# Weighed queries times both states as plain float32 products, without the splits of states and queries

## The chip, the core and the metric

The kernel runs on one core of a Trainium2 chip. Its engines are TensorE (PE, with its weight loads as PEld), VectorE (DVE), ScalarE (ACT), GpSimd (POOL) and SyncE (SP, which issues most DMAs). The metric is the device time of one execution in microseconds (us); lower is better.

## What is computed

One encoder block on x of 2048 tokens by 1024 channels: a norm, one input projection, two branches (a pooling mixer and a bidirectional mLSTM), a gate by SiLU for each, one output projection, the residual and a last norm. The change lies in the mLSTM. It has 4 heads of 256 channels and works in 16 chunks of 128 tokens, in two directions, with a state C (256 x 256) and n (256) that goes from chunk to chunk:

```python
def step(carry, xs):
    C, n, m = carry
    ...
    s = jnp.einsum('bhtd,bhsd->bhts', qj, kj) * jnp.exp(log_D - m_t[..., None])
    num = jnp.einsum('bhts,bhse->bhte', s, vj) + inter_w[..., None] * jnp.einsum('bhtd,bhde->bhte', qj, C)
    den = jnp.sum(s, axis=-1) + inter_w * jnp.einsum('bhtd,bhd->bht', qj, n)
    h = num / jnp.maximum(jnp.abs(den), jnp.exp(-m_t))[..., None]
    ...
    C_new = decay[..., None, None] * C + jnp.einsum('bhs,bhsd,bhse->bhde', ws, kj, vj)
```

## The kernel before

Most products are split: a float32 operand is cast to a high part of type fp32r, the low part is what is left, and a product of two operands becomes three one-pass products (high x high, high x low, low x high), summed in PSUM. Some products are plain float32 instead, among them the scores of the mLSTM (`sT`) and the headwise maps (`hw`).

The program has an input stage (all projections and small maps, results to DRAM), then the z blocks and the pooled branch, and then the mLSTM as a pipeline of 64 steps: step s is head h = s // 16, chunk j = s % 16 of the forward direction. The states of the backward direction are made one head ahead, one update for each step, and held in `cb`; the forward state is `cf`. Between the pieces of a step stand "fill" units, three passes each of the output projection (`po`).

A step uses these pieces. `weigh` multiplies the queries c by the weights of both states, for two directions and two halves of 128 channels (`cw`, on GpSimd). `weighed_high` and `weighed_low` split it (`cwh` on ScalarE, `cwl` on GpSimd). `state_high` and `state_low` split the state of direction d: `sh` on ScalarE, `sl` on DVE for the forward state (d = 0) and on GpSimd for the backward one (d = 1). `numerators` sums, per direction, the scores' part (`ph`, `pl` times `vh`, `vl`) and the states' part in one PSUM tile `num`, 258 columns wide. `denominators`, `ratio`, `moments`, `normalise`, `transposes`, `join`, `store` follow (`rn`, `hh`, `rstd`, `py`, `yt`). `forward` and `backward` update the states: six products into the PSUM tile `upd`, then DVE adds the decayed state (`cf`, `cb`). `upd` has one buffer (`psu`) for both directions, `cw` has two (`tp`).

The table `order` says what is done in iteration s, in the order of every engine: a piece, how many iterations it lags behind its step (`weigh` with -2 makes `cw` of step s + 2, `numerators` with 0 is step s) and sometimes the engine. For iterations up to 52 TensorE, DVE, ScalarE and GpSimd run exactly in this order; for the last steps the framework's scheduler orders all but TensorE. The first 53 iterations hold some five fill units each, later ones sixteen or fewer (`share`, `units`).

Of the kernel before, what the change touches and what calls it, by code (L numbers as in the profile page):

```python
# [10 lines left out]
F32 = mybir.dt.float32  # L11
# [6 lines left out]
P = 128  # L18
# [32 lines left out]
def hymba_block(ctx, tc, xT, x, w_in, wpxT, pool_w, bqT, bkT, bvT, bv, w_g, b_g, par, edge, w_out, g_out, out):  # L51
# [27 lines left out]
    # gate products that the recurrences use, token-major: column r = (dir, step, head)  # L79
# [16 lines left out]
    # ------------------------------------------------------------------ input projections  # L96
# [26 lines left out]
    # from the last z blocks on, TensorE runs in the order of the program  # L123
# [15 lines left out]
    # the small operands of the headwise maps, read ahead  # L139
# [3 lines left out]
    def load_headwise(i):  # L143
        t = {}
        for name, src in (("k", bkT), ("v", bvT)):
            t[name] = hwp.tile([P, P], F32, name=f"bl{name}")
            nc.sync.dma_start(out=t[name], in_=src[i])
        # the map of q and, beside it, the gates' weights of k, q and v
        t["q"] = hwp.tile([P, P + 48], F32, name="blq")
        nc.sync.dma_start(out=t["q"][:, :P], in_=bqT[i])  # L150
        nc.sync.dma_start(out=t["q"][:, P:].rearrange("p (a b) -> p a b", a=3), in_=w_g[i])
        t["vw"] = hwp.tile([P, 16 + P], F32, name="vw")
        nc.sync.dma_start(out=t["vw"][:, 16:], in_=bv[i])
        return t
# [6 lines left out]
    # W_poolx times the group's mix: pooling commutes with the mix of the channels  # L161
# [44 lines left out]
    with ExitStack() as pro:  # L206
        xq = open_pool(pro, "xq", bufs=2)

        # u is x g in two parts that one pass each carries; the row factor 1 / rms multiplies the products
# [40 lines left out]
        # the array's clock rises while the first loads run  # L250
# [38 lines left out]
    # ---- the mLSTM's inputs  # L289
    with pm:  # L290
# [5 lines left out]
        def prepare(i):  # L296
            bl, vw = hw[i], hw[i]["vw"]
            wq = bl["q"]
            # the columns of a map: what it adds to the gates, then its outputs
# [21 lines left out]
        def headwise(i, b):  # L321
# [3 lines left out]
            for src, off, rhs, dst in ((c, 0, mws[i], kk_s), (mxs[i], 2 + b * BT, hw[i]["vw"], v_s)):  # L325
                # v's columns end with ones, whose product with the keys is the denominator, and a pad
# [85 lines left out]
    # ---- z of the mLSTM (first heads) beside the gates: columns of gacc are (i|f, dir, head)  # L412
    with ExitStack() as pz:
# [31 lines left out]
        # in the order (dir, step, head)  # L445
# [15 lines left out]
        # rows r, columns t  # L461
# [34 lines left out]
        flat = lambda t: t.rearrange("p a b c -> p (a b c)")  # noqa: E731  # L496
# [30 lines left out]
    # ---- the pooling mixer  # L527
# [43 lines left out]
    # ------------------------------------------------------------------ mLSTM  # L571
# [9 lines left out]
    # keys and values of chunk j, and their parts; the keys carry the weights of the state's update  # L581
# [7 lines left out]
    # pieces of the split of keys and values  # L589
# [36 lines left out]
    # the state that chunk j - 1 receives from its right  # L626
# [25 lines left out]
    # ---- the output projection: units of three products, and chores that go between them  # L652
# [67 lines left out]
    def fillers():  # L720
        # the first and the last tiles go in pairs by halves of the columns, while the other half's weights come
# [9 lines left out]
        def ahead(i):  # L731
            # reads y of piece i when it can be had
            if i < len(pieces) and keys[i] not in ys and (pieces[i][0] == 0 or pieces[i][2] in done):
                ys[keys[i]] = load_y(*keys[i])
# [44 lines left out]
    # ---- a step of the forward direction, in pieces that go to different engines  # L779
# [20 lines left out]
    def mask(a):  # L800
        # keys s (partitions) that a query t may see: s <= t forward, s >= t backward
        for d, (pat, cm) in enumerate(((1, -1), (-1, 1))):
            nc.gpsimd.affine_select(out=a["gw"][:, 0, d, :], in_=a["gw"][:, 0, d, :], compare_op=ALU.is_ge, fill=BIG,
                                    base=0, pattern=[[pat, P]], channel_multiplier=cm)

    # c times the weights of the states, and its parts
# [5 lines left out]

    def weighed_high(a):
        a["cwh"] = tp.tile([P, 2, 2, P], F32R, name="cwh")
        nc.scalar.copy(a["cwh"][:, a["ds"]], a["cw"][:, a["ds"]])  # L815

    def weighed_low(a, eng):
        ds = a["ds"]
        a["cwl"] = tp.tile([P, 2, 2, P], F32R, name="cwl")
        eng.tensor_tensor(a["cwl"][:, ds], a["cw"][:, ds], a["cwh"][:, ds].bitcast(F32), op=ALU.subtract)  # L820
# [24 lines left out]
    def numerators(a):  # L845
# [6 lines left out]
        for d in a["dirs"][::-1]:  # L852
            sh, sl = a["sh", d], a["sl", d]
            for m in range(2):
                for n, (l, r) in enumerate((("cwh", sh), ("cwh", sl), ("cwl", sh))):
                    pe(nc.tensor.matmul(num[:, d, :E], lhsT=a[l][:, d, m, :], rhs=r[:, m, :],
                                        start=False, stop=(m == 1 and n == 2)))

    # the parts of the state that step a meets in direction d
    def state_high(a, d):  # L860
        if d in a["dirs"]:
            a["state", d] = cb.pop((a["h"], a["j"])) if d else a["cf"]
            a["sh", d] = fp.tile([P, 2, E], F32R, name=f"sh{d}", bufs=1)
            nc.scalar.copy(a["sh", d], a["state", d])  # L864

    def state_low(a, d, eng):
        if d in a["dirs"]:
            a["sl", d] = fp.tile([P, 2, E], F32R, name=f"sl{d}", bufs=1)
            eng.tensor_tensor(a["sl", d], a["state", d], a["sh", d].bitcast(F32), op=ALU.subtract)  # L869
# [72 lines left out]
    # most of the pooled half's products go evenly into the first FULL steps  # L942
# [9 lines left out]
    def behind(s):  # L952
        # the backward update of the next head that goes with step s
# [3 lines left out]
    # ---- z of the last heads, beside the first backward states; each block that is done makes room  # L957
    for pair in ((4,), (5,), (6, 7)):
# [29 lines left out]
    # The steps run as a pipeline. What is done in iteration s, in the order of every engine: a piece, how many  # L988
    # iterations it lags behind its step, and for some the engine
    V, G = nc.vector, nc.gpsimd  # L990
    order = (
        ("store", 3, V), ("scores_low", 0, G), ("denominators_2", 1), ("state_high_0", 0), ("ratio_0", 1),
        ("forward", 0), ("back_values_high", -1), ("state_low_0", 0, V), ("ratio_1", 1), ("normalise_1", 2),
        ("fill", 0), ("fill", 0), ("state_low_1", 0, G), ("moments_0", 1), ("weighed_low", 0, G), ("fill", 0),
# [4 lines left out]
        ("back_values_low", -1, V), ("skip", 1), ("denominators_1", 0), ("weighed_high", -1), ("state_high_1", -1),  # L999
        ("scores_high", -1),  # L1000
# [4 lines left out]
        mask=mask, weigh=weigh, weighed_high=weighed_high, weighed_low=weighed_low, exponentials=exponentials,  # L1005
# [3 lines left out]
    for n, piece in (("state_high", state_high), ("state_low", state_low), ("denominators", denominators),  # L1009
                     ("moments", moments), ("normalise", normalise)):  # L1010
# [4 lines left out]
    def run(span):  # L1015
        for s in span:
# [7 lines left out]
            # products of the output projection that go into this iteration  # L1024
# [31 lines left out]
# ---- layout of the inputs, and the launch on one core  # L1056
# [48 lines left out]
```

## Time and profile before

| | us |
|---|---|
| three runs | 1572.33, 1572.82, 1577.58 (median 1572.82) |
| profiled execution: span from the first to the last instruction | 1570.6 |
| what lies around the span, against the median | 2.2 |
| busy in the span: PE | 1477.8 (94%) |
| PEld | 1257.9 (80%) |
| DVE | 1034.2 (66%) |
| ACT | 650.6 (41%) |
| POOL | 624.6 (40%) |

Busy time is the time in which an engine has an instruction at work, its waits for a memory port included. Matmuls are pipelined: one's end overlaps the next, so the distance from start to start is what a product costs in a row, and the busy time of a lone matmul is longer. The stages differ much in which engine is full; a share over the whole span mixes them.

### The profile page before, as it was taken

The page shows a single profiled execution, that of the slowest core. Times are in us where ns is not written, and L with a number is a line of the kernel's source. Part 1 is how long each engine was busy: PE and PEld are TensorE (multiplying, and loading weights), DVE is VectorE, ACT ScalarE, POOL GpSimd, SP SyncE. Part 2 cuts the span into 40 slices and gives each one's busy share as a digit, 9 for nine tenths or more (in the row PEclk, how much of TensorE's full clock was granted, in tenths as well). Part 3 has the DMA queues.
Part 4 walks back from the last instruction along what each step waited for, and adds up shares of the span by engine and source line. Part 5 has one row for each costly group of instructions (what it writes and reads, how often), then busy time and mean ns, then how long its engine had stood idle before and what let it go on. Part 6 is the DMA issues. An engine that isn't in the chain of part 4 may idle for free.

```text
span 1570.6 us, 23151 instructions
## 1 busy us (share of the span) xinstructions
PE 1477.8 (94%) x7801; PEld 1257.9 (80%) x7801; DVE 1034.2 (66%) x1993; ACT 650.6 (41%) x1516; POOL 624.6 (40%) x752
## 2 busy tenths in 40 slices
PE   8899999999999999999999888888888899899998
PEld 6689888878888888888887777777777777787886
DVE  8795445562134333434543999999999999766753
ACT  6245443442011110001234666666666666635431
POOL 6543333310000222221020777777767778443300
PEclk9999999999999999999999999999999999999999
DMA  6268766542111101111337776676676667754352
GB/s 218 73 201 242 184 182 177 167 143 77 55 54 54 54 16 52 54 54 54 101 108 226 235 200 185 203 207 189 193 208 192 187 202 239 203 181 154 119 163 81
DMA packets 251351, 231.25 MB, mean 147 GB/s; under 512 B 18400, under 2 KB 211168, under 8 KB 250208
## 3 DMA queue, kind: packets, MB, share of 16 engines
q1 hardware_dynamic: 236768, 215.08, 45.9%
q10 hardware_dynamic: 14464, 14.68, 3.0%
q8 instruction: 62, 1.02, 0.3%
q14 instruction: 57, 0.47, 0.1%
HBM read 149.81 MB, written 79.89 MB: 146 GB/s over the span
## 4 chain that ended last, share of the span: by engine, by line
PE 56%; DVE 22%; DMA 8%; POOL 6%; issue 5%; ACT 3%; SPq 1%; POOLq 0%; DVEq 0%; ACTq 0%
PE proj L135 40%; PE po L704 7%; PE hw L336 4%; DVE yt L936 3%; DVE rstd L907 2%; DVE vl L605 2%; DMA gw<-g_s 2%; DVE cb L622 1%; DMA ym_s<-yt 1%; DVE yt L931 1%; PE hw L185 1%; DVE sl L869 1%; POOL cwl L820 1%; DVE kl L596 1%; POOL cw L810 1%
## 5 line engine op out<-in xcount | busy, mean ns | idle before, releaser
L135 PE MATMUL proj<-uh,whi 128*128 128x512 f32 x1024 | 403.8, 395 | 4.6 <-DVE mx L204 3.6
L135 PE MATMUL proj<-ul,whi 128*128 128x512 f32 x1024 | 401.5, 392 | 1.5 <-DVE ul L218 1.5
L135 PE MATMUL proj<-uh,wlo 128*128 128x512 f32 x1024 | 401.8, 393 | 0.4 <-DVE wlo L94 0.4
L135 PEld LDWEIGHTS proj<-uh,whi 128*128 128x128 f32 x1024 | 193.7, 189 | 43.3 <-DVE mx L204 3.7
L135 PEld LDWEIGHTS proj<-uh,wlo 128*128 128x128 f32 x1024 | 193.4, 189 | 41.7 <-DVE wlo L94 0.8
L135 PEld LDWEIGHTS proj<-ul,whi 128*128 128x128 f32 x1024 | 193.6, 189 | 40.9 <-DVE ul L218 2.6
L704 PE MATMUL po<-woh,yh 128*128 128x512 f32 x512 | 205.7, 402 | 3.2 <-DVE o L707 1.8
L704 PE MATMUL po<-woh,yl 128*128 128x512 f32 x512 | 202.4, 395 | 2.3 <-DVE yl L94 2.3
L704 PE MATMUL po<-wol,yh 128*128 128x512 f32 x512 | 202.0, 395 | 1.2 <-DVE wol L94 1.2
L91 ACT CAST whi<-wl 128x1024 fp32r<-128x1024 f32 x31 | 32.6, 1052 | 228.7 <-PE proj L135 225.5
L704 PEld LDWEIGHTS po<-woh,yl 128*128 128x128 f32 x512 | 96.6, 189 | 25.2 <-DVE yl L94 3.1
L616 PE MATMUL upd<-vh,kh 128*128 128x258 f32 x240 | 72.6, 302 | 46.8 <-ACT vh L601 45.1
L704 PEld LDWEIGHTS po<-woh,yh 128*128 128x128 f32 x512 | 96.7, 189 | 22.3 <-DVE o L707 2.4
L704 PEld LDWEIGHTS po<-wol,yh 128*128 128x128 f32 x512 | 96.8, 189 | 19.2 <-DVE wol L94 1.5
L316 DVE SCALAR_TENSOR_TENSOR c<-mx,par_sb,c 128x512 f32<-128x512 f32 x128 | 103.4, 825 | 3.0
L543 DVE TENSOR_TENSOR ux<-proj,rnorm 128x512 f32<-128x512 f32 x32 | 22.1, 691 | 124.7 <-PE proj L135 124.7
L869 POOL TENSOR_TENSOR sl<-cb,sh 128x516 fp32r<-128x516 f32 x60 | 86.5, 1441 | 29.9 <-ACT sh L864 25.4
L810 POOL TENSOR_TENSOR cw<-cT,gw 128x512 f32<-128x512 f32 (+1 forms) x64 | 91.8, 1434 | 7.8 <-DMA gw<-g_s 5.7
L556 POOL TENSOR_TENSOR win<-ux 128x2063 f32<-128x2063 f32 x8 | 29.0, 3624 | 160.7 <-DVE ux L543 160.7
L820 POOL TENSOR_TENSOR cwl<-cw,cwh 128x512 fp32r<-128x512 f32 (+1 forms) x64 | 90.3, 1411 | 6.4 <-ACT cwh L815 4.9
L616 PEld LDWEIGHTS upd<-vh,kh 128*128 128x128 f32 x240 | 45.2, 188 | 55.9 <-ACT hh L884 51.5
L843 POOL TENSOR_TENSOR pl<-dd,ph 128x256 fp32r<-128x256 f32 x64 | 51.4, 804 | 87.4 <-ACT ph L839 87.4
(216 smaller groups left out, 3187.4 us busy)
## 6 DMA issues: line engine op xcount, KB each, us to landing
gw<-g_s SPq DMA_DIRECT2D x128, 128.0 KB, 4.4
v<-v_s SPq DMA_DIRECT2D x124, 129.0 KB, 3.4
kk<-kk_s SPq DMA_DIRECT2D x124, 128.0 KB, 3.6
wl<-in_w_in SPq DMA_DIRECT2D x23, 512.0 KB, 3.9
xt<-in_xT SPq DMA_DIRECT2D x32, 256.0 KB, 4.1
cT_s<-c SPq DMA_DIRECT2D x32, 256.0 KB, 3.6
kk_s<-tokst SPq DMA_DIRECT2D x32, 256.0 KB, 2.6
kkT_s<-kkTb SPq DMA_DIRECT2D x32, 256.0 KB, 4.1
```

The costliest lines, as they stand in the source:

```text
L91: nc.scalar.copy(hi, src)
L135: pe(nc.tensor.matmul(ps, lhsT=l[:, kt, :], rhs=r[:, kt, :], start=(kt == 0 and n == 0), stop=(kt == KT - 1 and n == 2)))
L316: nc.vector.scalar_tensor_tensor(c, in0=mx[:, b * BT + t:(b + 1) * BT + t], scalar=par_sb[:, i, t:t + 1], in1=c, op0=ALU.mult, op1=ALU.add)
L336: nc.tensor.matmul(ps[:, e, :], lhsT=src[:, o:o + P], rhs=rhs, start=True, stop=True)
L605: eng.tensor_tensor(t["vl"], t["v"], t["vh"].bitcast(F32), op=ALU.subtract)
L616: pe(nc.tensor.matmul(ps[:, m, :E], lhsT=t[l][:, ms], rhs=t[r_], start=(n == 0), stop=(n == 2)))
L704: pe(nc.tensor.matmul(ps, lhsT=l[:, kt, :], rhs=r, start=(kt == 0 and e == 0), stop=(kt == 7 and e == 2)))
L810: eng.tensor_tensor(a["cw"][:, ds], a["cT"][:, None].broadcast_to([P, nd, 2, P]), a["gw"][:, 1, ds, None, :].broadcast_to([P, nd, 2, P]), ...
L820: eng.tensor_tensor(a["cwl"][:, ds], a["cw"][:, ds], a["cwh"][:, ds].bitcast(F32), op=ALU.subtract)
L843: eng.tensor_tensor(a["pl"], a["dd"], a["ph"].bitcast(F32), op=ALU.subtract)
L869: eng.tensor_tensor(a["sl", d], a["state", d], a["sh", d].bitcast(F32), op=ALU.subtract)
L936: eng.tensor_tensor(yt, yt, a["sz"], op=ALU.mult)
```

## The change

`numerators` multiplies `cw` and the states themselves, as plain float32 products, two for a direction (one for each half). The casts and subtractions that split them are gone from `order` and from the program. Nothing else of the table is moved; the rest of the diff takes out comments.

```diff
-    def weighed_high(a):
-        a["cwh"] = tp.tile([P, 2, 2, P], F32R, name="cwh")
-        nc.scalar.copy(a["cwh"][:, a["ds"]], a["cw"][:, a["ds"]])
-
-    def weighed_low(a, eng):
-        ds = a["ds"]
-        a["cwl"] = tp.tile([P, 2, 2, P], F32R, name="cwl")
-        eng.tensor_tensor(a["cwl"][:, ds], a["cw"][:, ds], a["cwh"][:, ds].bitcast(F32), op=ALU.subtract)
...
         for d in a["dirs"][::-1]:
-            sh, sl = a["sh", d], a["sl", d]
+            state = cb.pop((a["h"], a["j"])) if d else a["cf"]
             for m in range(2):
-                for n, (l, r) in enumerate((("cwh", sh), ("cwh", sl), ("cwl", sh))):
-                    pe(nc.tensor.matmul(num[:, d, :E], lhsT=a[l][:, d, m, :], rhs=r[:, m, :],
-                                        start=False, stop=(m == 1 and n == 2)))
-
-    # the parts of the state that step a meets in direction d
-    def state_high(a, d):
-        if d in a["dirs"]:
-            a["state", d] = cb.pop((a["h"], a["j"])) if d else a["cf"]
-            a["sh", d] = fp.tile([P, 2, E], F32R, name=f"sh{d}", bufs=1)
-            nc.scalar.copy(a["sh", d], a["state", d])
-
-    def state_low(a, d, eng):
-        if d in a["dirs"]:
-            a["sl", d] = fp.tile([P, 2, E], F32R, name=f"sl{d}", bufs=1)
-            eng.tensor_tensor(a["sl", d], a["state", d], a["sh", d].bitcast(F32), op=ALU.subtract)
+                pe(nc.tensor.matmul(num[:, d, :E], lhsT=a["cw"][:, d, m, :], rhs=state[:, m, :],
+                                    start=False, stop=(m == 1)))
...
-        ("store", 3, V), ("scores_low", 0, G), ("denominators_2", 1), ("state_high_0", 0), ("ratio_0", 1),
...
+        ("store", 3, V), ("scores_low", 0, G), ("denominators_2", 1), ("ratio_0", 1),
...
```

The programs of both kernels show where instructions now stand. GpSimd in a step of the pipeline's middle, before; `[waits ...]` names the engines and DMA queues that an instruction waits for, and the PE that `sl` waits for is the last reader of the part of the state that it replaces:

```order
L843 TENSOR_TENSOR pl<-dd,ph 128x256 [waits Activation_49]
L869 TENSOR_TENSOR sl_9902<-cb,sh_9856 128x516 [waits PE_49]
L820 TENSOR_TENSOR cwl<-cw,cwh 128x512
L803 AFFINE_SELECT gw<-gw 128x128 [waits DMAHW4_49]
L803 AFFINE_SELECT gw<-gw 128x128
L902 TENSOR_TENSOR rstd<-rstd,mhalf 128x1 [waits DVE_49]
L810 TENSOR_TENSOR cw<-cT,gw 128x512 [waits DMAHW7_49,Pool_49]
```

GpSimd in a like step of the changed kernel (`pl` is now line 834, the power for `rstd` line 880):

```order
L803 AFFINE_SELECT gw<-gw 128x128 [waits DMAHW2_49]
L803 AFFINE_SELECT gw<-gw 128x128
L880 TENSOR_TENSOR rstd<-rstd,mhalf 128x1 [waits DVE_49,Pool_49]
L810 TENSOR_TENSOR cw<-cT,gw 128x512 [waits DMAHW4_49,DMAHW5_49,PE_49,Pool_49]
L834 TENSOR_TENSOR pl<-dd,ph 128x256 [waits Activation_49,Pool_49]
```

`sl` and `cwl` are gone from between `pl` and the mask, and `cw` now waits for PE: it is written into the buffer that the numerators of this same iteration read, and they stand behind it in the table.

TensorE at the numerators of an early step of the pipeline, as a piece of the difference (- before, + changed; a row with x2 is the two halves of a direction):

```order
-L856 MATMUL num<-sh_7031,cwh 128x258
-L856 MATMUL num<-sl_7046,cwh 128x258
-L856 MATMUL num<-sh_7031,cwl 128x258
+L841 MATMUL num<-vh,ph 128x258
+L841 MATMUL num<-vl,ph 128x258
+L841 MATMUL num<-vh,pl 128x258
+L841 MATMUL num<-vh,ph 128x258
+L841 MATMUL num<-vl,ph 128x258
+L841 MATMUL num<-vh,pl 128x258
+L846 MATMUL num<-cb,cw 128x258 x2
+L846 MATMUL num<-cf,cw 128x258 x2
 L616 MATMUL upd<-vh,kh 128x258
```

The scores' part stays (its line number alone changes), and the states' part shrinks from twelve products to four, in the same place, ahead of the forward update.

## Rows read from the trace of the kernel before

**Rows 1.** The page: busy time by engine, and DVE's busy tenths in 40 slices

```profile
PE 1477.8 (94%) x7801; PEld 1257.9 (80%) x7801; DVE 1034.2 (66%) x1993; ACT 650.6 (41%) x1516; POOL 624.6 (40%) x752
...
DVE  8795445562134333434543999999999999766753
```

**Rows 2.** Busy time by stretch: start:end length, engines (instructions), clock, DMA share, GB/s

```profile
870.00:1326.00 456.00, 397.35 (x2461) 347.80 (x2462) 450.70 (x1043) 297.56 (x761) 330.18 (x358) 1.00 0.70 202
1326.00:1376.00 50.00, 44.56 (x220) 36.64 (x220) 41.61 (x85) 32.76 (x81) 28.62 (x32) 0.93 0.73 205
1376.00:1481.00 105.00, 102.88 (x540) 87.28 (x539) 72.86 (x184) 48.73 (x131) 39.09 (x46) 1.00 0.51 161
```

**Rows 3.** Waits of PE from 870 to 1326 us: total us, times, longest

```profile
PE upd L616 <- ACT vh L601: 45.1, 40, 1.7
PE py L920 <- ACT hh L910: 5.1, 7, 1.7
PE upd L616 <- DVE kl L596: 4.3, 8, 1.0
```

**Rows 4.** Timeline of one step: start us, duration us, engine, line, [idle before <- releaser]

```profile
1241.51 1.47 POOL L869 TENSOR_TENSOR sl<-cb,sh 128x516 fp32r<-128x516 f32 x1
...
1241.83 1.44 DVE L936 TENSOR_TENSOR yt<-yt,sz 128x256 f32<-128x256 f32 x1
...
1242.17 0.61 PE L830 MATMUL sT<-cT,kkT 128*128 128x128 f32 x4
1242.94 1.45 POOL L820 TENSOR_TENSOR cwl<-cw,cwh 128x512 fp32r<-128x512 f32 x1
...
1243.26 0.73 DVE L622 SCALAR_TENSOR_TENSOR cf<-cf,dec_bc,upd 128x516 f32<-128x516 f32 x1
...
1244.14 0.36 PE L616 MATMUL upd<-vh,kh 128*128 128x258 f32 x1 [1.36 <-ACT vh L601]
...
1246.61 0.39 DVE L605 TENSOR_TENSOR vl<-v,vh 128x258 fp32r<-128x258 f32 x1
...
1247.67 1.64 POOL L810 TENSOR_TENSOR cw<-cT,gw 128x512 f32<-128x512 f32 x1
...
1247.93 0.28 PE L856 MATMUL num<-sh,cwl 128*128 128x258 f32 x1
...
1248.04 1.28 DVE L907 SCALAR_TENSOR_TENSOR rstd<-mv,rstd 128x1 f32<-128x1 f32 x1
...
1248.76 0.40 PE L704 MATMUL po<-woh,yh 128*128 128x512 f32 x1
...
1250.17 0.73 POOL L843 TENSOR_TENSOR pl<-dd,ph 128x256 fp32r<-128x256 f32 x1 [0.87 <-ACT ph L839]
...
1251.57 0.61 PE L830 MATMUL sT<-cT,kkT 128*128 128x128 f32 x4
```

**Rows 5.** Groups by line, 870 to 1326 us: busy us, mean ns, idle before

```profile
L810 POOL TENSOR_TENSOR cw<-cT,gw 128x512 f32<-128x512 f32 (+1 forms) x51 | 74.9, 1468 | 0.0
...
L869 POOL TENSOR_TENSOR sl<-cb,sh 128x516 fp32r<-128x516 f32 x49 | 71.8, 1466 | 0.0
...
L869 DVE TENSOR_TENSOR sl<-cf,sh 128x516 fp32r<-128x516 f32 x49 | 51.6, 1054 | 0.0
L803 POOL TENSOR_SCALAR_AFFINE_SELECT gw<-gw 128x128 f32<-128x128 f32 x104 | 49.4, 496 | 0.7 <-ACT sh L864 0.7
```

**Rows 6.** The stretch 870 to 1326 us, line 856 alone: PE, PEld, clock, DMA

```profile
870.00:1326.00 456.00, 77.38 (x576) 72.54 (x576) 1.00 0.70 202
```

**Rows 7.** Tile `yt`, from 870 to 1326, then 1376 to 1481: min/median/max ns

```profile
L936 DVE TENSOR_TENSOR yt<-yt,sz x50: 407/1435/1480, 892.4 to 1324.7; 128x256 f32<-128x256 f32 x50
...
L936 DVE TENSOR_TENSOR yt<-yt,sz x7: 413/425/427, 1388.6 to 1478.8; 128x256 f32<-128x256 f32 x7
```

**Rows 8.** Timeline of PE in the input stage: plain products of 144 columns

```profile
310.40 1.14 PE L336 MATMUL hw<-mw,c 128*128 128x144 f32 x8
```

More of the change, by code (lines that the diff above doesn't have):

```diff
@@ L991, in hymba_block @@
     order = (
-        ("store", 3, V), ("scores_low", 0, G), ("denominators_2", 1), ("state_high_0", 0), ("ratio_0", 1),
-        ("forward", 0), ("back_values_high", -1), ("state_low_0", 0, V), ("ratio_1", 1), ("normalise_1", 2),
-        ("fill", 0), ("fill", 0), ("state_low_1", 0, G), ("moments_0", 1), ("weighed_low", 0, G), ("fill", 0),
+        ("store", 3, V), ("scores_low", 0, G), ("denominators_2", 1), ("ratio_0", 1),
+        ("forward", 0), ("back_values_high", -1), ("ratio_1", 1), ("normalise_1", 2),
+        ("fill", 0), ("fill", 0), ("moments_0", 1), ("fill", 0),
         ("mask", -2), ("fill", 0), ("values_high", -1), ("moments_1", 1), ("keys_high", -2), ("values_low", -1, V),
@@ L998, in hymba_block @@
         ("numerators", 0), ("back_keys_high", -1), ("back_keys_low", -1), ("join", 2), ("denominators_0", 0),
-        ("back_values_low", -1, V), ("skip", 1), ("denominators_1", 0), ("weighed_high", -1), ("state_high_1", -1),
-        ("scores_high", -1),
+        ("back_values_low", -1, V), ("skip", 1), ("denominators_1", 0), ("scores_high", -1),
     )
@@ L1004, in hymba_block @@
         values_high=lambda t: values_high(t["kv"]), values_low=lambda t, e: values_low(t["kv"], e),
-        mask=mask, weigh=weigh, weighed_high=weighed_high, weighed_low=weighed_low, exponentials=exponentials,
+        mask=mask, weigh=weigh, exponentials=exponentials,
         scores=scores, weigh_scores=weigh_scores, scores_high=scores_high, scores_low=scores_low,
@@ L1008, in hymba_block @@
         transposes=transpose_step, join=join, store=store_step)
-    for n, piece in (("state_high", state_high), ("state_low", state_low), ("denominators", denominators),
-                     ("moments", moments), ("normalise", normalise)):
+    for n, piece in (("denominators", denominators), ("moments", moments), ("normalise", normalise)):
         pieces.update({f"{n}_{k}": lambda t, *e, k=k, piece=piece: piece(t, k, *e) for k in range(4)})
```

## The prediction

> **What bounds the kernel now.** I began with the page's busy shares. TensorE is busy for 94% of the span and VectorE (DVE) for 66%, but the row of slices shows DVE at nine tenths or more in a run of slices from just past the middle to about five sixths [rows 1]. That run is the pipelined mLSTM, so an average over the span says little, and I cut it into stretches [rows 2]. From 870 to 1326 us DVE is busy for 450.7 of 456.0 us and PE for 397.4: PE idles 58.65 us. From 1376 on PE is busy for 102.9 of 105 us and DVE for 72.9. So the first stretch belongs to DVE, the later one to PE, and one edit can be worth something different in each. The list of PE's waits in the first stretch [rows 3] puts 45.1 of its 58.65 us on one place: the first product of a state update, 40 times, up to 1.7 us. Two smaller waits hang on DVE's results too (5.1 and 4.3 us).
>
> The timeline of one step shows what is late there [rows 4]. PE has finished the scores at 1242.17 + 0.61 and then stands until 1244.14. The view names ScalarE's cast of v, but one PSUM buffer (`psu`, one buffer) serves both updates: the backward one can't start before DVE has read the forward one into `cf`, and that read runs from 1243.26 to 1243.99. It is late because DVE's store product `yt` in front of it took 1.44 us, from 1241.83 to 1243.27, and GpSimd's `sl` had begun just before it and ended at 1242.98. The same product takes 0.43 us in the stretch where GpSimd has little to do, against a median of 1.44 here [rows 7]; `rstd`, one column wide, takes 1.28 and ends with GpSimd's `cw`, at 1249.3 [rows 4]. `cf`, which reads PSUM, keeps 0.73 while `cwl` runs [rows 4]. So a DVE operation with both inputs in SBUF waits until the GpSimd operation that began first is through. The Trainium skill says this as a rule (SBUF — State Buffer, Who interferes with whom: an instruction of DVE with two SBUF inputs contends with one of GpSimd that reads SBUF, and the loser blocks for its whole length); the trace agrees, with the two times of `yt`.
>
> A step takes 9.12 us (456.0 over 50 stores [rows 2, 7]) and PE has 7.95 us in it.
>
> **What the change costs on PE.** Three split products per direction and half become one plain float32 product: 2 directions x 64 steps, less 8 ends, x 2 halves = 240 products, 192 of them in the first stretch (576 records over 3) [rows 6]. One split pass of 258 columns takes 0.12 us: from the last numerator to the first output product there are 7 starts in 0.83 us [rows 4]. A plain product of this width is not in the trace. The score products are plain, and 2 of them leave 4 records [rows 4], so a product is two records. Four records of 128 columns last 0.61 us, eight of 144 columns 1.14 [rows 4, 8]; less one drain of 0.28 (a lone record's length) that is 0.110 and 0.123 us a record, 0.86 and 0.85 ns a column. At 258 columns: 0.22 a record, 0.44 a product, against 3 x 0.12 = 0.36. So +0.08 us each: 15.4 us in the first stretch, 3.8 us behind it. The lower bound is a record at the price of one split pass (0.24 a product, 29 us saved in all); 0.123 for a mere 144 columns speaks against it. The upper bound is two split passes a record, 0.48, or 29 us lost in all. I take 0.44, since both plain rows agree on the price per column. The Trainium skill has the rule that speaks against the change (FP8 and Floating Point Precision, TensorE Precision Notes: true float32 is four passes through the array): four against three. The row's pass of 0.12 makes that 0.48, the upper bound, and the sum below would end 10 us later.
>
> **What it takes away.** DVE loses `sl` of the forward state, 1.05 us [rows 5]. GpSimd loses `sl` of the backward state (1.47 [rows 5]) and `cwl` (1.45 [rows 4]), some 2.9 of 6.6 us busy a step (330.2 over 50 [rows 2]). ScalarE loses three casts; it is busy for 297.6 of 456 us [rows 2] and ends nothing, so they count as nothing. If `yt` no longer meets `sl`, it falls from 1.44 to 0.43. DVE's 9.0 us a step (450.7 over 50) become about 7.0, below PE's 7.95 + 0.31 = 8.26. PE becomes the last engine of the stretch, and the gain is bounded by its 58.65 us of idling less the 15.4 that it now has to do more.
>
> **The wait that the change adds.** PE now reads `cw` itself, at the end of a step, where before ScalarE and GpSimd had read it at the start. `cw` has two buffers, so the next but one can only be written when this step's numerators are through; the order of GpSimd shows it as a wait on PE in front of `cw`. Behind `cw` stand `pl` (0.73) and the mask, and on DVE whatever needs two SBUF inputs: first `vl`, then `yt`, then (in DVE's order) `cf`. I walk it with t = 0 at the start of the last numerator record. Result at 0.4 (0.28 for a split record, and some more for a wider one, an estimate); `cw` 0.5 to 1.97 (mean 1.47 [rows 5]); `vl` behind it to 2.36 (0.39 [rows 4]); `pl` may get in before `yt`, to 3.09; `yt` to 3.52; the reciprocal and `cf` (0.73) to about 4.3; PE sees it at 4.4, or at 3.7 if `yt` is ahead of `pl`. PE has other work until then: the record itself 0.22, the forward update 6 x 0.12 = 0.72, twelve output products 2.81 (1248.76 to 1251.57), the scores 4 x 0.11 [rows 4]: 4.2 us. So PE waits between nothing and 0.2 us; I take 0.1 a step, 5 us. `rstd`, in turn, no longer has `cw` beside it.
>
> **The sum for the first stretch.** PE's 397.4 us; + 15.4 for the plain products; - 6.4, since each of 40 waits that goes also hides a drain (0.28 counted as busy, where the next start follows at 0.12); + 5 of new waiting; + 8.9 of the other waits (58.65 - 45.1 = 13.55, and half of the 9.4 us that hang on DVE's lateness goes). That is 420.3 against 456.0: 35.7 us saved, a step of 8.4 us. Behind 1326 us PE is nearly full, with 5.4 us idle between 1326 and 1376 and 2.1 in the next 105 [rows 2]; I give no gain there, and 48 x 0.08 = 3.8 us are lost. Ahead of the mLSTM nothing is changed. Net 32 us. The profiled execution spans 1570.6 us, 2.2 below the runs' median of 1572.8, which has what lies around the span; I carry that over: 1572.8 - 32 = 1541.
>
> **Rivals.**
> No change (0.12). The new wait replaces the old one. If one of the mask's two records (0.50 each [rows 5]) also gets in before `yt`, PE sees `cf` at 4.9 and waits 0.7 us a step. The step is then 8.26 - 0.13 (the drains) + 0.18 (the other waits) + 0.7 = 9.0; the 5.5 us saved and the 3.8 lost give 1571, with 1565 to 1580 around it. For it: `cw` now begins exactly where DVE's short chain begins. Against it: the mask also needs its loads, and DVE, with 1.2 us in hand a step, can be at `yt` before GpSimd is through with `pl`.
> Slower (0.08). Both mask records get in, PE sees `cf` at 5.4 and waits 1.2 us a step, nearly the 1.36 of now, and every plain product is paid in full on top: a step of 9.5, 20 us lost in the first stretch and 3.8 behind it, 1597 (1607 at 0.48 a product). It decides at a wait of 0.9 us, that is `cf` at 5.1. For it: GpSimd's order has the mask right behind `pl`, so one late `yt` lets all of it through. Against it: the old wait had a 1.5 us operation that is gone.
> More gain (0.10). All of PE's waits that hang on DVE go, and the walk's 0.2 us never show: 397.4 - 6.4 + 15.4 + 4 = 410, 46 us less, net 42: 1531; with the plain record below 0.22, to 1520. For it: DVE is the only engine with no idle time in the stretch.
> The forecast has 0.70, its own range 1531 to 1556 (a price of 0.48 and a wait of 0.2 us together add 15).
>
> **Numbers.** 1541 us. The range 1520 to 1567 takes in the larger gain and reaches to the edge of no change; what lies outside is the slower case and most of no change. What a measurement of this kernel tells from no change is about 0.5%, 7.9 us: faster (below 1565) 0.81, within it 0.11, slower 0.08.
>
> **What would show it.** Right: `yt` near 0.43 us or at least under 1 us, DVE below full in the stretch and PE near 97%, the wait before the backward update under 0.3 us a step, steps of about 8.4 us, records of `num` from `cw` starting 0.22 us apart, `cw` beginning right behind the numerators, `vl` stretched. Wrong: a start-to-start well off 0.22 (the price), `yt` or `vl` at 1.4 us with `cf` late (the new wait), or DVE still full although `sl` is gone. It would also be wrong if loads become the limit: the DMA share is 0.70 [rows 2], and steps 8% shorter bring it to 0.76.

## The result, and the profile after

The changed kernel takes 1524.69 us (median of 4 runs, 1523.34 to 1529.47) against 1572.88 (4 runs, 1572.33 to 1577.58) of the kernel before on the same chip: a ratio of 0.9692, 95% interval 0.9673 to 0.9711. That is 48 us less, where 32 were forecast; the range held it. The profiled execution of the changed kernel was the slowest of its four (1529.47), so its rows explain 42.8 of the 48.2 us (a span of 1527.8 us against 1570.6).

The page of the changed kernel, busy time by engine and DVE's slices [rows 1]:

```profile
PE 1475.6 (97%) x7561; PEld 1256.7 (82%) x7561; DVE 912.8 (60%) x1933; ACT 555.0 (36%) x1332; POOL 423.8 (28%) x628
...
DVE  8796355563133333445445397778888886766653
```

DVE's run of nines is gone; PE is busy for 2 us less, DVE for 121 us less. By stretch, cut at the same places of the program as [rows 2]:

```profile
870.00:1283.00 413.00, 393.08 (x2262) 345.67 (x2262) 343.17 (x992) 219.98 (x613) 167.54 (x256) 1.00 0.77 222
1283.00:1333.00 50.00, 46.84 (x226) 38.87 (x225) 33.56 (x83) 28.76 (x74) 11.35 (x20) 0.97 0.74 209
1333.00:1438.00 105.00, 102.95 (x507) 86.47 (x507) 71.55 (x182) 40.60 (x117) 26.03 (x40) 1.00 0.54 167
```

The first stretch went from 456 to 413 us, the later ones kept their length: all of the gain is where DVE was full. DVE is now busy for 83% there, PE for 95% (393.08 of 413). PE's waits in it [rows 3], total us, times, longest:

```profile
PE upd L616 <- DVE cf L622: 10.1, 9, 3.0
PE py L898 <- ACT hh L888: 7.7, 8, 1.9
PE upd L616 <- ACT woh L91: 1.3, 1, 1.3
PE sT L821 <- DVE dd L826: 0.4, 1, 0.4
```

The 40 waits before the backward update are nine. What is left comes seldom and is long, mostly 0.5 to 3 us. Among the waits of the other engines are two of ScalarE for DMAs that had been small in the kernel before (870 to 1326 us):

```profile
ACT yt L926 <- DMA ym_s<-yt: 19.9, 24, 2.3
...
ACT kh L592 <- DMA kk<-kk_s: 0.6, 2, 0.5
```

In the changed kernel (870 to 1283 us) they are large, and the new wait for the numerators is there:

```profile
ACT kh L592 <- DMA kk<-kk_s: 69.4, 36, 4.3
ACT yt L904 <- DMA ym_s<-yt: 66.0, 41, 3.4
...
POOL cw L810 <- PE num L846: 38.0, 22, 3.3
```

The timeline of a step at the numerators [rows 4], as there:

```profile
1213.41 1.04 PE L846 MATMUL num<-cb,cw 128*128 128x258 f32 x4
...
1214.29 1.03 PE L846 MATMUL num<-cf,cw 128*128 128x258 f32 x4
...
1215.46 1.48 POOL L810 TENSOR_TENSOR cw<-cT,gw 128x512 f32<-128x512 f32 x1 [0.92 <-PE num L846]
...
1216.29 0.94 DVE L605 TENSOR_TENSOR vl<-v,vh 128x258 fp32r<-128x258 f32 x1
...
1216.90 0.92 POOL L834 TENSOR_TENSOR pl<-dd,ph 128x256 fp32r<-128x256 f32 x1
...
1217.22 0.89 DVE L914 TENSOR_TENSOR yt<-yt,sz 128x256 f32<-128x256 f32 x1
...
1218.10 0.73 DVE L622 SCALAR_TENSOR_TENSOR cf<-cf,dec_bc,upd 128x516 f32<-128x516 f32 x1
```

The second group of four records starts 0.88 us after the first: 0.22 each, 0.44 a product. `cw` begins after the numerators; `vl` is stretched until `cw` is through, `yt` until `pl` is, then comes `cf`: the chain of the prediction, in its order. In this step `cf` is in time, and PE doesn't wait for it. Over the 50 steps that are cut below, `vl` takes more than 0.5 us in 16 of 95 cases and `yt` in 25 of 49; before it was 31 and 47. By tiles, min/median/max ns (from 870 to 1283 us) [rows 5, 7]:

```profile
L914 DVE TENSOR_TENSOR yt<-yt,sz x50: 407/877/1456, 893.7 to 1282.5; 128x256 f32<-128x256 f32 x50
...
L605 DVE TENSOR_TENSOR vl<-v,vh x96: 390/413/1459, 876.0 to 1279.6; 128x258 fp32r<-128x258 f32 x96
...
L885 DVE SCALAR_TENSOR_TENSOR rstd<-mv,rstd x51: 146/152/1285, 883.1 to 1280.9; 128x1 f32<-128x1 f32 x51
```

`yt`'s median fell from 1435 to 877, not to 430. `rstd`, which took 1.28 us in [rows 4], now takes 0.15.

For all kernels below I cut the pipeline at the first score record (`sT`) of each step: the 50 steps that the first stretch holds, the 11 after them, and the rest. "Waits" is the time in which no PE record is at work; "PE at work" is the remainder. All in us, worked out from the records of the profiled execution. The last column is TensorE's mean granted clock in the 50 and in the 11 steps, as a share of the higher of its two levels (1.2 and 2.4 GHz).

| kernel | before the 50 | 50 steps | waits | PE at work | DVE busy | 11 steps | rest | clock |
|---|---|---|---|---|---|---|---|---|
| before | 873.2 | 445.1 | 58.7 | 386.4 | 440.3 | 162.7 | 89.5 | 1.000 / 0.979 |
| changed | 873.9 | 402.7 | 18.6 | 384.1 | 336.0 | 161.3 | 89.8 | 0.996 / 0.989 |
| e1 | 872.4 | 432.1 | 36.9 | 395.2 | 420.6 | 169.0 | 90.3 | 0.988 / 1.000 |
| e2 | 871.0 | 396.2 | 23.0 | 373.2 | 354.0 | 159.6 | 89.4 | 0.996 / 0.989 |
| e3 | 874.7 | 402.5 | 19.2 | 383.3 | 365.9 | 169.9 | 90.5 | 0.996 / 0.970 |
| e4 | 871.8 | 396.8 | 11.3 | 385.5 | 365.7 | 158.0 | 90.5 | 0.996 / 0.989 |
| e5 | 875.2 | 398.0 | 16.0 | 382.0 | 353.6 | 161.3 | 89.8 | 1.000 / 1.000 |
| e6 | 873.8 | 381.9 | 3.7 | 378.2 | 350.1 | 159.3 | 90.1 | 0.996 / 0.979 |
| e7 | 871.8 | 422.2 | 3.3 | 418.9 | 348.7 | 168.2 | 90.7 | 0.992 / 1.000 |
| e8 | 872.8 | 446.4 | 33.0 | 413.4 | 435.2 | 166.2 | 91.0 | 1.000 / 0.990 |
| e9 | 876.0 | 448.9 | 62.7 | 386.2 | 442.8 | 160.6 | 89.5 | 1.000 / 0.989 |
| e10 | 873.5 | 376.7 | 8.3 | 368.4 | 356.5 | 153.8 | 89.5 | 0.991 / 1.000 |
| e11 | 872.0 | 393.8 | 13.7 | 380.1 | 363.9 | 163.7 | 89.9 | 0.991 / 0.969 |
| e12 | 872.5 | 388.0 | 8.4 | 379.6 | 357.5 | 158.1 | 89.4 | 0.991 / 0.978 |

What the lower level costs can be read in e3. PE idles for 4.07 us in front of the first line below; the clock is at the lower level on both sides of that wait (granted 0.51 of the higher one from 1300 to 1310 us), and output products start 0.42 us apart, later 0.23:

```profile
1305.92 0.80 PE L704 MATMUL po<-woh,yl 128*128 128x512 f32 x1 [4.07 <-DVE yl L94]
...
1309.08 0.63 PE L704 MATMUL po<-woh,yh 128*128 128x512 f32 x1
1309.50 0.63 PE L704 MATMUL po<-wol,yh 128*128 128x512 f32 x1
...
1310.61 0.40 PE L704 MATMUL po<-wol,yh 128*128 128x512 f32 x1
1310.84 0.39 PE L704 MATMUL po<-woh,yl 128*128 128x512 f32 x1
```

So a clock of 0.99 in place of 1.00 can cost up to 4 us in the 50 steps and 1.6 in the 11, and differences between rows of that size may be the clock's.

### The profile page after: what moved, and what is told of

Same layout as the page of the kernel before. It is cut to its first block, busy times and chain, and to the rows that moved or that the text cites. A ratio compares the mean times of both kernels' runs of the same rounds, so it can differ in the third digit from the quotient of the medians.

```text
span 1527.8 us, 22436 instructions
## 1 busy us (share of the span) xinstructions
PE 1475.6 (97%) x7561; PEld 1256.7 (82%) x7561; DVE 912.8 (60%) x1933; ACT 555.0 (36%) x1332; POOL 423.8 (28%) x628
## 4 chain that ended last, share of the span: by engine, by line
PE 63%; DMA 16%; DVE 9%; ACT 6%; issue 4%; POOL 2%; SPq 1%; POOLq 0%; DVEq 0%; ACTq 0%
PE proj L135 40%; PE po L704 11%; DMA ym_s<-yt 5%; DMA kk<-kk_s 5%; PE hw L336 4%; PE num L846 2%; PE upd L616 2%; PE hw L185 1%; DVE vl L605 1%; DMA wost<-in_w_out 1%; PE num L841 1%; DVE yt L914 1%; PE hw L344 1%; DVE yt L909 1%; DMA gw<-g_s 1%
## 5 line engine op out<-in xcount | busy, mean ns | idle before, releaser
L810 POOL TENSOR_TENSOR cw<-cT,gw 128x512 f32<-128x512 f32 (+1 forms) x64 | 82.8, 1294 | 84.1 <-issue 38.3
L592 ACT ACTIVATE kh<-kk,ws_tok 128x256 fp32r<-128x256 f32 x124 | 62.3, 504 | 103.6 <-DMA kk<-kk_s 75.8
L616 PE MATMUL upd<-vh,kh 128*128 128x258 f32 x240 | 82.6, 344 | 11.6 <-DVE cf L622 10.1
L880 POOL TENSOR_TENSOR rstd<-rstd,mhalf 128x1 f32<-128x1 f32 x64 | 36.0, 563 | 166.3 <-DVE rstd L878 160.3
L904 ACT ACTIVATE yt<-cT,par_sb 128x128 f32<-128x128 f32 x128 | 44.4, 394 | 85.1 <-DMA ym_s<-yt 85.1
L204 DVE TENSOR_TENSOR mx<-proj,rnorm 128x512 f32<-128x512 f32 x32 | 21.7, 688 | 87.3 <-PE proj L135 83.5
```

The costliest lines, as they stand in the source:

```text
L592: nc.scalar.activation(t["kh"], t["k"], AF.Copy, scale=ws_tok[:, t["r"]:t["r"] + 1])
L616: pe(nc.tensor.matmul(ps[:, m, :E], lhsT=t[l][:, ms], rhs=t[r_], start=(n == 0), stop=(n == 2)))
L810: eng.tensor_tensor(a["cw"][:, ds], a["cT"][:, None].broadcast_to([P, nd, 2, P]), a["gw"][:, 1, ds, None, :].broadcast_to([P, nd, 2, P]), ...
L880: nc.gpsimd.tensor_tensor(a["rstd"][:, 0:1], a["rstd"][:, 0:1], mhalf[:, :1], op=ALU.pow)
L904: nc.scalar.activation(a["yt"][:, m, :], a["cT"][:, m, :], AF.Copy, scale=par_sb[:, i, 8:9])
```

## The experiments

The first question was which part of the edit paid; the second, what the remaining waits are; the third, what each price was. Beside runs e1 to e4 the kernel before took 1573.02 us, beside e5 to e8 1574.82, beside e9 to e12 1574.02; each ratio is to the one beside it, and times of different groups compare to about 2 us.

**e1: plain products alone.** The kernel before, its splits still made and read by no one.

```diff
-                for n, (l, r) in enumerate((("cwh", sh), ("cwh", sl), ("cwl", sh))):
-                    pe(nc.tensor.matmul(num[:, d, :E], lhsT=a[l][:, d, m, :], rhs=r[:, m, :],
...
+                pe(nc.tensor.matmul(num[:, d, :E], lhsT=a["cw"][:, d, m, :], rhs=state[:, m, :],
```

> The kernel before, with its products of queries and states made plain; all splits of states and queries are still computed, though nothing reads their results. Port theory (the gain is the relief of DVE and GpSimd, which block each other; the plain products only cost TensorE time): DVE stays full, its 1.17 us of idle TensorE a step hides the dearer products, 1573 us (1565 to 1590). Rival (the gain is TensorE's: fewer products and weight loads): near the changed kernel, 1525 to 1545.

Measured 1565.72 us, ratio 0.9949 (0.9932 to 0.9967). PE's waits, from 870 to 1270 us:

```profile
PE upd L616 <- DVE cf L622: 24.4, 21, 2.4
PE upd L616 <- DVE kl L596: 1.9, 2, 1.0
```

DVE is still busy for 420.6 of 432.1 us and stays the bound. Some 7 us come without any of the work removed. What differs on the other engines is that `cw` now starts behind the numerators in all 50 steps (before, it starts ahead of their end in 46), and `yt`'s median in this run is 1003 ns; that this pays the 7 us is likely, but not shown. So about 41 of the 48 us hang on the operations removed from DVE, GpSimd and ScalarE.

**e2: no low parts.** The kernel before without `sl` and `cwl`; PE makes its three passes with the high parts.

```diff
-            sh, sl = a["sh", d], a["sl", d]
+            sh = a["sh", d]
...
-                for n, (l, r) in enumerate((("cwh", sh), ("cwh", sl), ("cwl", sh))):
+                for n, (l, r) in enumerate((("cwh", sh), ("cwh", sh), ("cwh", sh))):
```

> The kernel before without the low parts of states and queries: the three subtractions on DVE and GpSimd are left out, and TensorE makes its twelve split passes with the high parts alone, so the output lacks the low parts' share. Port theory: all of the relief without the dearer products, so 240 x 0.07 = 17 us below the changed kernel's 1525: 1508 (1498 to 1522). Rival (TensorE's own gain): 1573, as nothing changes on TensorE.

Measured 1519.48 us, ratio 0.9661 (0.9646 to 0.9676): the removal alone gives the whole gain and 5 us more. But the price of the plain products (17 us) would have put it near 1508. PE waits here too, 23.0 us in the 50 steps, most of it in front of `py`:

```profile
PE py L920 <- ACT hh L910: 11.4, 13, 1.4
PE upd L616 <- ACT vh L601: 5.9, 12, 1.2
```

`yt`'s median is 415 ns, so the GpSimd collisions that I had in mind can't be what holds this kernel. Something else does, and it showed as ScalarE's waits for DMAs (870 to 1270 us):

```profile
ACT yt L926 <- DMA ym_s<-yt: 48.4, 40, 3.5
...
ACT kh L592 <- DMA kk<-kk_s: 24.2, 25, 2.0
```

**e3 and e4: one engine's work back.** The changed kernel, with GpSimd's two subtractions put back (e3), or DVE's one (e4), their results unread.

```diff
+            low = fp.tile([P, 2, E], F32, name=f"low{d}", bufs=1)
+            eng.tensor_tensor(low, state, state, op=ALU.subtract)
...
+        eng.tensor_tensor(low[:, ds], a["cw"][:, ds], a["cw"][:, ds], op=ALU.subtract)
...
-        ("fill", 0), ("fill", 0), ("moments_0", 1), ("fill", 0),
+        ("fill", 0), ("fill", 0), ("keep_state_1", 0, G), ("moments_0", 1), ("keep_queries", 0, G), ("fill", 0),
```

> The changed kernel with GpSimd's two subtractions put back in their old places, reading the state and cw and writing tiles that nothing reads; DVE's subtraction and the casts stay out. Port theory: the store product on DVE waits behind them again (1.4 us), the state's read of PSUM comes late, TensorE waits 0.4 to 0.9 us a step: 1545 to 1570. Rival (DVE's own subtraction was what counted): 1525 to 1532.

> The changed kernel with DVE's one subtraction put back in its old place, its result unread; GpSimd's two stay out. Port theory: DVE has 6.9 us a step and TensorE 8.06, so 0.6 to 1.0 us more fits: 1525 to 1538. Rival (DVE's own subtraction was what counted): 1550 to 1573.

e3 took 1540.22 us (0.9795; 0.9779 to 0.9811), e4 1517.53 (0.9647; 0.9626 to 0.9669). GpSimd's work costs 15.5 us, less than I had thought. DVE's costs nothing; e4 is even 7 us faster than the changed kernel, with 30 us more DVE work and 7 us less waiting. Both theories missed that: the amount of work on DVE isn't what leaves PE waiting now. The two don't add up to the 41 us that e1 leaves: with one of them back DVE is busy for 91 or 92% of the 50 steps, with all three subtractions and the casts (e1) for 97%. It takes them together to make DVE the bound again.

**e5: a third buffer for `cw`,** to take away the new wait.

```diff
-        a["cw"] = tp.tile([P, 2, 2, P], F32, name="cw")
+        a["cw"] = tp.tile([P, 2, 2, P], F32, name="cw", bufs=3)
```

> The changed kernel with a third buffer for cw, so that GpSimd's weighing of the queries no longer waits for TensorE's numerators (38 us of GpSimd's waits in the changed kernel's long stretch). Theory, that this new wait is what leaves cf late and TensorE waiting 10 us for it: those waits go and the time falls by 5 to 10 us, 1515 to 1520. Rival, from the kernel that kept the splits and still gained 7 us: the wait does good, since it puts GpSimd's weighing where VectorE writes little to SBUF; with a third buffer yt or rstd is stretched again and the time stays or rises, 1523 to 1535.

Measured 1525.34 us (0.9691; 0.9668 to 0.9714), the same as the changed kernel. The theory falls. `yt`'s median is 416 ns, but `rstd` is back at 1232 ns (152 in the changed kernel), as the rival had it: `cw` runs beside it again. So the edit takes one hold-up away and brings another, and PE still waits for the same two things:

```profile
PE upd L616 <- DVE cf L622: 7.5, 12, 1.0
PE py L898 <- ACT hh L888: 6.1, 7, 1.5
```

**e6: a third buffer for keys, values and `yt`.** In the changed kernel the chain in front of one of PE's waits reads, in the timeline:

```profile
1204.36 2.17 SPq L586 DMA_DIRECT2D v<-v_s  x1
1206.58 0.43 SPq L915 DMA_DIRECT2D ym_s<-yt  x1
...
1209.53 0.70 ACT L904 ACTIVATE yt<-cT,par_sb 128x128 f32<-128x128 f32 x2 [3.43 <-DMA ym_s<-yt]
...
1210.43 0.46 ACT L862 ACTIVATE hh<-num,rn 128x256 f32<-128x256 f32 x1
...
1210.92 0.48 DVE L866 SCALAR_TENSOR_TENSOR hh<-num,rn,hh 128x256 f32<-128x256 f32 x1 [1.30 <-ACT hh L862]
1211.09 0.60 ACT L888 ACTIVATE hh<-hh,rstd 128x256 f32<-128x256 f32 x1
...
1211.74 0.44 PE L898 MATMUL py<-ident,hh 128*128 128x128 f32 x2 [0.96 <-ACT hh L888]
```

`yt` has two buffers. In `order` its store (lag 3) stands at the head of a row, and `skip` (lag 1), in which ScalarE writes the same buffer for the next tile but one, at the end of that row. The transfers have also become slower: the times of these stores from issue to landing, first before (870 to 1326 us), then in the changed kernel (870 to 1283 us):

```profile
DMA to landing us min/median/max: 1.9/3.2/5.2
DMA to landing us min/median/max: 2.5/4.3/6.5
```

ScalarE stands still for the store, and with it all that is queued behind: `ph`, `hh`, and so PE's `py`. The store itself comes behind a load of values that holds SyncE for 2.17 us, where most loads in this view take 0.3 to 0.5.

```diff
-        k = pool.tile([P, HD], F32, name="kk", bufs=2)
+        k = pool.tile([P, HD], F32, name="kk", bufs=3)
...
-        v = pool.tile([P, E], F32, name="v", bufs=2)
+        v = pool.tile([P, E], F32, name="v", bufs=3)
...
-        a["yt"] = tp.tile([P, 2, P], F32, name="yt")
+        a["yt"] = tp.tile([P, 2, P], F32, name="yt", bufs=3)
```

> The changed kernel with three buffers in place of two for the loaded keys and values and for the tile yt that is stored at a step's end. In the changed kernel ScalarE waits 69 us for the load of the keys and 66 us for the store of yt in the long stretch. Theory, that these transfers now end last in the steps in which TensorE still waits (py for hh, the update for cf): both ScalarE waits shrink below half, TensorE's idle time in the long stretch falls from about 20 us to about 10, and the time is 1512 to 1519. Rival: ScalarE has slack and its waits cost nothing, 1522 to 1528.

Measured 1505.83 us (1503.71 to 1506.89), ratio 0.9564 (0.9546 to 0.9583): 19 us under the changed kernel, more than the theory's best. Both ScalarE waits are gone from the list. The first 400 us of the pipeline by engine, and PE's waits from 870 to 1283 us (the 50 steps end at 1256, and the two rows of `po` lie behind them):

```profile
870.00:1270.00 400.00, 396.31 (x2312) 352.73 (x2311) 362.44 (x1006) 224.39 (x629) 176.75 (x263) 1.00 0.80 234
```

```profile
PE upd L616 <- DVE cf L622: 3.0, 1, 3.0
PE po L704 <- DVE yl L94: 1.8, 1, 1.8
PE po L704 <- ACT yh L91: 1.2, 1, 1.2
PE py L898 <- ACT hh L888: 0.6, 1, 0.6
```

PE is busy for 99%. The DMA share rose from 0.77 to 0.80: the transfers could go faster than the changed kernel let them, and what lacked was buffers to cover the latency. Which of the three tiles paid isn't separated. And `yt` has a median of 1046 ns here: a slow `yt` costs nothing as long as `cf` is in time.

**e7 and e8: half of the states' products twice,** in the changed kernel and in the one before.

```diff
+                for again in range(2 - m):
+                    pe(nc.tensor.matmul(num[:, d, :E], lhsT=a["cw"][:, d, m, :], rhs=state[:, m, :],
...
-                for n, (l, r) in enumerate((("cwh", sh), ("cwh", sl), ("cwl", sh))):
+                for n, (l, r) in enumerate((2 - m) * (("cwh", sh), ("cwh", sl), ("cwl", sh))):
```

> The changed kernel with the product of half 0 of the weighed queries and the state done twice in both directions, so the numerators count that half twice; 120 more plain products, two records of 258 columns each. It measures their price in a kernel that TensorE is said to bound. Theory, TensorE is the bound and a product takes 0.435 us (start to start of its records 0.217 us): 52 us of work, of which the idle time that is left absorbs at most 10, 1567 to 1577. At the 0.24 us that the lower bound of the prediction had: 1550 to 1555. Rival, another engine bounds the changed kernel: under 1545.

> The kernel before with the three passes of half 0 done twice in both directions, so the numerators count that half twice; 360 more passes of 258 columns at 0.12 us, 43 us of work for TensorE, 36 us of them in the long stretch. Theory, VectorE bounds the long stretch of the kernel before and TensorE's 58 us of idle time there take most of the new work: 1575 to 1592. Rival, TensorE bounds it and its idle time is forced by a chain through it: 1605 to 1617.

e8 took 1578.97 us, ratio 1.0033 (1.0023 to 1.0043): 43 us of new PE work cost 4. The 50 steps are 1.3 us longer, with 25.7 us less waiting; DVE stays the bound:

```profile
870.00:1320.00 450.00, 416.84 (x2699) 372.64 (x2697) 437.98 (x1023) 292.08 (x746) 318.82 (x347) 1.00 0.69 202
```

e7 took 1555.78 us (0.9884; 0.9866 to 0.9902): 31 us more than the changed kernel for 52 us of work, between the two expectations, and just above the 1550 to 1555 that a product of 0.24 us would have given. The reason is not a cheaper product. This kernel's 50 steps hold 3.3 us of PE's waiting, about as e6's do: ScalarE still waits 55.6 us for the store and 15.3 for the keys, but in a step that is 0.4 us longer none of it reaches PE. Against e6, the run without waits, it is 50.0 us slower, and PE at work in the 50 steps is 418.9 - 378.2 = 40.7 us more for 94 more products (564 records against 376): 0.433 us a product. The clock (0.992 and 0.996) may hold up to 2 us of the 40.7, but the records say the same: in both runs they start 0.217 to 0.218 us apart at the median.

**e9 and e10: three buffers in other kernels.** e9 is the kernel before with three buffers for keys and `yt`, e10 is e2 with those of e6; the edits are the ones shown.

> The kernel before with three buffers for the loaded keys and for the tile yt (the values keep two, there is no room for more). In the changed kernel three buffers for keys, values and yt were worth 19 us. Theory: in the kernel before VectorE is the bound, the transfers are not what ends last, and nothing is won: 1567 to 1576. Rival: the transfers hold the kernel before just as much, and part of the change's gain could have been had without it: 1550 to 1560.

> The kernel before without the low parts (TensorE keeps its three passes a product, all of the high parts, so the low parts are left out of the numerators), with three buffers for the loaded keys and values and for yt. TensorE has the old work, VectorE and GpSimd the new. Beside the changed kernel with three buffers (1506) it gives what the plain products cost TensorE, once no engine or transfer is in the way. The prediction's price, 0.08 us more a product: 240 products make 19 us, 1487. By the start-to-start times, 0.434 against three times 0.120 to 0.123: 16 to 18 us, 1488 to 1490. By the whole stretch of the changed kernel, 8 us there and some 3 later: 1495. If another engine or a transfer is still in the way of both: 1500 to 1507.

e9 took 1574.57 us, ratio 1.0005 (0.9993 to 1.0016): nothing, as expected of a kernel that DVE bounds. Its PE still waits at the old place:

```profile
PE upd L616 <- ACT vh L601: 43.7, 39, 1.7
```

e10 took 1496.12 us (0.9504; 0.9488 to 0.952), 23 us under e2. So 10 us lie between e6 and e10, where the start-to-start times gave 16 to 18. In the steps in which PE never waits the price is the predicted one: at the median 7.03 and 7.76 us for e10's steps of 12 and 15 output products, 7.35 and 8.07 for e6's, 0.31 to 0.32 us for four products, 0.08 each. The other steps hide part of it: e10 waits 4.6 us more than e6 in the 50. The clock blurs the rest: in the 11 later steps it was 1.000 in e10 and 0.979 in e6, which may be up to 3.4 of the 5.5 us between them there.

**e11 and e12: what of GpSimd hurts.** e6 with GpSimd's two subtractions back (e11), or with a memset of 128x1650 in place of each (e12).

```diff
-            eng.tensor_tensor(low, state, state, op=ALU.subtract)
+            low = fp.tile([P, 1650], F32, name="low", bufs=1)
+            eng.memset(low, 0.0)
```

> The changed kernel with three buffers for keys, values and yt, and GpSimd's two subtractions of the splits back (their results are not read). Theory, GpSimd's operations stretch VectorE's writes wherever they meet, and VectorE with them comes near its bound: yt's median rises above 1.1 us, cf comes late again, and the time is 1515 to 1530. Rival, VectorE has slack enough (its busy share of the stretch is under 0.92) and TensorE stays full: 1505 to 1510, whatever yt takes.

> As the run with GpSimd's two subtractions, but each is a memset of 128x1650, which writes and reads nothing, of about the same length. Theory, what stretches VectorE is GpSimd's being in SBUF with two operands: memsets do it no harm, yt's median stays at 0.9 us, and the time is 1505 to 1510. Rival, any GpSimd operation of that length does the same, by what it writes or by what it holds up behind it on GpSimd: as the run with subtractions, within 4 us.

e11 took 1523.86 us (0.9676; 0.9661 to 0.9691), 18.0 over e6; e12 1510.02 (0.9591; 0.9576 to 0.9605), 4.2 over it, although a memset takes 1.48 us and a subtraction here 1.04 to 1.15 on average. The same place in both timelines, first e11:

```profile
1197.48 1.26 POOL L817 TENSOR_TENSOR low<-cb 128x516 f32<-128x516 f32 x1
...
1197.83 1.19 DVE L925 TENSOR_TENSOR yt<-yt,sz 128x256 f32<-128x256 f32 x1
...
1198.71 1.22 POOL L822 TENSOR_TENSOR cwlow<-cw 128x512 f32<-128x512 f32 x1
...
1199.03 0.72 DVE L622 SCALAR_TENSOR_TENSOR cf<-cf,dec_bc,upd 128x516 f32<-128x516 f32 x1
```

and e12:

```profile
1193.02 1.48 POOL L816 MEMSET low<- 128x1650 f32 x1
...
1193.39 0.41 DVE L923 TENSOR_TENSOR yt<-yt,sz 128x256 f32<-128x256 f32 x1
...
1193.80 0.73 DVE L622 SCALAR_TENSOR_TENSOR cf<-cf,dec_bc,upd 128x516 f32<-128x516 f32 x1
```

`yt` begins 0.35 us after GpSimd's operation in both. Beside the subtraction it takes 1.19 us, to 0.28 us past the subtraction's end; beside the memset 0.41, as if GpSimd were idle. That holds for each of the 10 and 11 times that `yt` begins beside one in the 50 steps (1.19 to 1.20, and 0.405 to 0.409). `cf`, which reads PSUM, takes 0.72 to 0.75 beside any. So it is GpSimd's reading that blocks DVE, and only DVE's operations with both inputs in SBUF. The Trainium skill says so (SBUF — State Buffer, Who interferes with whom: a DVE instruction with two SBUF inputs contends with a GpSimd instruction that reads SBUF and not with one that only writes it); the two rows agree. The 14 us between e11 and e12 hold more than these ten cases: in e11 `yt` also begins beside `cw` in 25 of the 50 steps (1.44 us at the median), in e12 in four.

## Why the prediction came out as it did

**Right: the bound, the cause, the place.** DVE bounded the first stretch (e8: PE could take in 43 us of work for 4; e9: more buffers for the transfers won nothing), the update's wait for `cf` was the thing lost, and the removal of `sl` and `cwl` took it away (e2, against e1). "A step of about 8.4 us" came out at 8.05 (402.7 over 50), the wait before the update at 0.2 us a step (10.1 over 50), records of `num` 0.22 apart.

**Right: the price of a plain product.** 0.44 was taken; e7 against e6 gives 0.433, and the full steps of e6 and e10 give +0.08 against three passes. By the Trainium skill (FP8 and Floating Point Precision, TensorE Precision Notes) true float32 is four passes; at the split pass of 0.12 that is 0.48, an estimate that the measurement doesn't bear out. The measurement doesn't speak against four passes, though: four in 0.433 us would be 0.108 each. What failed is to price them as split passes; how many there are these runs don't show.

**Wrong in size: "each of 40 waits that goes also hides a drain", 6.4 us.** e10 and the kernel before give PE the same instructions. In the 50 steps PE is at work for 386.4 us in the one, with 58.7 us of waiting, and for 368.4 in the other, with 8.3. So the waits cost 18.0 us more than their own length. The clock doesn't make this: it was 1.000 in the one and 0.991 in the other, so at one clock the 18.0 would be larger, by up to 3.4. By distances from start to start, less the idle time, the last score record of a step, which the update follows, accounts for 6.8 us of it (12.6 to 5.8): this is the drain of the prediction. The last record of `py` (6.0 to 1.3) and the updates' own records (65.0 to 59.7) add 10.0, which it didn't have: waits shorter than the drain before them, which the list of waits doesn't show, and slow first records behind a wait. In the changed kernel the term is 386.4 + 188 x 0.08 - 384.1 = 17.3 us.

**Wrong: "the wait that the change adds", 5 us.** The chain is there as walked, but it doesn't cost 0.1 us in each step: PE waits for `cf` nine times, 10.1 us in all. e5 takes the wait for the numerators away and wins nothing, so that wait isn't a net loss: `cw` had begun ahead of the numerators' end, with `rstd` beside it in 42 of 50 steps (1.27 us at the median), and in the changed kernel `rstd` meets it in 3 of 50.

**Wrong: what the remaining waits are.** 13.9 us were forecast, 9.7 of them as DVE's lateness; 18.6 are there, and e6 removes 14.9 of them, and 19 us of time, with buffers. That loads could become the limit was named, but by the DMA share; the limit was latency against two buffers. Before, a step was 1 us longer and the same store landed after 3.2 us in place of 4.3, and ScalarE waited 19.9 us for it in place of 66.0.

**The sum.** In the 50 steps PE's work was to rise by 9.0 (15.4 - 6.4) and fell by 2.3; waiting was to fall by 44.8 and fell by 40.1. Together 42.4 saved in place of 35.7. Behind them 3.8 were to be lost; 11 steps and rest are 1.1 shorter (the clock, 0.979 and 0.989 in the 11, may hold up to 1.6 of it). Ahead, 0.7 more. That is 42.8 against 32, and most of the rest of the 48.2 is the profiled execution, 4.8 us over its median. The result lies past the forecast and past the rival "more gain" at 1531. The range reached down to 1520 for the sake of a plain record below 0.22 us, and that is not what happened: the records were priced right, the term of the drains was 10.9 us too small and that of the remaining waits 4.7. That the result is still inside the range is in part luck.

**Open.** Why e4, with a DVE operation more, waits 7 us less than the changed kernel. It shifts ScalarE and DVE against the transfers, and with two buffers a step's waits hang on such shifts, but I didn't run e4 with three buffers. In e4 `yt` takes 0.43 us at the median, so the added operation also moved it away from GpSimd's; but in e5 it takes 0.42, and PE waits 16.0 us all the same. The loss of e3 lies by the profile mostly in the 11 later steps (169.9 against 161.3): PE waits 12.0 us there against 6.5, and the clock (0.970 against 0.989) may hold some 3 us more. Why the later steps lose by GpSimd's work I didn't test.

## What to carry to other kernels

When an engine that was full gets room, ask at once which latency the old step had been covering: here third buffers were worth nothing before the change (e9, for keys and `yt`) and 19 us after it (e6, for the values too; 69 us under the kernel before, the fastest run here that leaves nothing out). Count the time of a wait as more than its length, since records around it fill and drain. And leaving out a split is worth what it takes off the engine that bounds, as long as the engine that does the product has room to pay for it: PE paid 0.08 us a product more, and the kernel still gained 3%.

## What the runs showed of the hardware

- A plain float32 product of 128x128 by 258 columns is two records, 0.217 us from start to start each, 0.433 a product when PE is full (e7 against e6); a split pass of the same shape takes 0.12.
- A DVE operation with two SBUF inputs that begins while GpSimd reads SBUF ends 0.28 us after GpSimd's; beside a memset it keeps its 0.41 us (`yt` in e11 and e12). With one input in PSUM it keeps its time beside either (`cf`, 0.72 to 0.75 us).
- 58.7 us of PE waiting, in 83 pieces of over 0.05 us, made PE's other work 18.0 us longer (before against e10, same instructions for PE).
- 43 us of new PE work cost 4 us in the kernel that DVE bounds (e8), 52 us cost 31 in the one with waits for transfers (e7 against the changed kernel), and 50 against the one without them (e6).
- While TensorE's granted clock was at the lower of its two levels, output products of 512 columns started 0.42 us apart in place of 0.23 (e3, at 1309 and 1310 us).
